# One gate's tile is computed ahead of the factor of the low-rank keys, in place of the attention's filling

## The chip, the cores and the metric

The kernel runs on one core of a Trainium2 chip. Five engines work side by side, each through its own queue in order: TensorE (PE) multiplies, its weight loads (PEld) overlap the products; VectorE (DVE) and ScalarE (ACT) do elementwise work; GpSimd (POOL) does a little; SyncE (SP) issues the transfers. They wait for each other at semaphores. The metric is the device time of one execution in microseconds.

## The reference

Two layers of an encoder trunk on 512 tokens of width 1024, in float32. Cut to what matters here:

```python
h = rms_norm(x, norm_mix[l])
u = h @ w_in[l]                    # queries, keys, values of three attentions, low-rank paths, gates
ya = prefix_block_attention(qa, ka, va, True, cum_logf)         # branch 0
qb = rms_norm(qd, mla_q_norm[l]) @ w_q_up[l]
kvb = rms_norm(kvd, mla_kv_norm[l]) @ w_kv_up[l]                # keys and values from 256 features
yb = prefix_block_attention(q_mla, k_mla, vb, False)            # branch 1
yc = chunk_band_attention(qc, kc, vc, rel_bias[l])              # branch 2
proj = einsum('bsnc,ncd->bsnd', y, w_branch[l])
gates = sigmoid(gl + b_gate[l])    # gl: 3 x 1024 columns of u
x = x + (gates * proj).sum(2) @ w_out[l]
h = rms_norm(x, norm_ffn[l])
x = x + square(relu(h @ w_ff1[l])) @ w_ff2[l]
```

## The kernel before, in words

**Products.** A float32 operand is split into a rounded high part and the rest: weights into `whi` (a copy by ACT, L142) and `wlo` (a subtraction by DVE, L143), and each product is three passes of TensorE, high by high, high by low, low by high. A weight tile of 128x1024 arrives in `raw` (L139, a load by SP). `raw`, `whi` and `wlo` have a ring of three buffers each, so a new tile can be copied only when the products of an older one are done.

**One layer.** The mixer runs the attention of branch 0, then of branch 2, then of branch 1 (the low-rank one), and after each attention its branch products `ps_b` (L803). The feed-forward part follows.

**Filling.** An attention is a generator that yields between its steps: scores S (`ps_s`, L683), probabilities P (transposes `ps_p` L713, copied by ACT to `pth` L715, low half by DVE to `ptl` L716), values V (`ps_y`, L726), transposes T (`ps_q`, L585, copied by ACT L587 and DVE L588 to `st`). It yields an amount of time, and `fill.run` takes that much of work that does not depend on it: the gate tiles. A gate tile (`gate`, by `win_tile`) is eight steps of three products (`ps_f`, L334), 650 ns of debt each, and behind the last an evacuation (DVE L778, ACT L779) and a store to `gd`. Branch 1's attention has eight such tiles; `ready` scales its debts so that eight tiles just fill it. The last head's steps have a larger weight (`tail`), so the end is filled most.

**The low-rank stage.** Before that attention its queries and keys are made, and the third branch's products (of branch 2) are woven in. The order is written out by hand as a string, `TUNE["mla"]`, one letter after the other: d and u are the low-rank tiles of queries and of keys (two steps for a letter), 0 and 1 the two scale factors, q and k the products from the low-rank features to queries, and to keys and values (`ps_t`, L369), b the branch products, t one step of the attention ahead of time (its first two are the transposes of queries and of keys), g one step of filling. It is read by these lines:

```python
            for c in TUNE["mla"]:
                if c == "t":
                    next(at)
                elif c == "g":
                    fill.run(650.0)
                elif c in "01":
                    self.mla_factor(int(c), st)
                    work["qk"[int(c)]] = (self.mla_q, self.mla_kv)[int(c)](l, st), 3 - int(c)
                else:
                    for _ in range(work[c][1]):
                        next(work[c][0], None)
```

A factor (`mla_factor_`, L478 on) is a sum over features on TensorE (`ps_sum`, L294), then some twelve small operations of DVE that end in `mf` (L485). The evacuation of a queries' or keys' tile (ACT L492 and L494, DVE L496) needs `mf`. When all four keys' tiles are evacuated, DVE makes a scale from their sums (L536, then the steps of `rsqrt`, L253 to L257) and multiplies the keys by it (L542); then they are transposed (the second t). The values' tiles, from the same products, are evacuated by ACT L412 and DVE L413. The branch products' results are taken by DVE L811 and L812.

**Order.** TensorE follows the program's order. On the other engines a scheduler sorts the instructions by priority when the program is built; after that each queue is fixed.

**Start.** `TUNE["warm"]` products of 128 columns (`ps_warm`, L1018) run while the first loads arrive.

Of the kernel before, what the change touches and what calls it, by code (L numbers as in the profile page):

```python
# [59 lines left out]
KTAGS = ("y", "s", "s", "mm")  # L60
TUNE = dict(

    mla='ddddddddddddubuubu0qqqbbqqqqqbbuuuubqbbb1kbbktkkkbbbkkkbtbbgg',

    over=[1.0, 1.0, 1.0],

# [1 line left out]

    tv=[13, 24],

    warm=15,

    st=[0, 2, 4],

# [1061 lines left out]
```

## Time and profile before

| | us |
|---|---|
| median of 3 runs | 1815.14 |
| lowest and highest | 1812.81, 1815.45 |
| the profiled execution, its time | 1812.97 |
| the profiled execution, its span | 1811.2 |
| PE busy | 1790.6 (99%) |
| DVE busy | 1078.2 (60%) |
| ACT busy | 783.8 (43%) |
| POOL busy | 88.8 (5%) |

The mean granted clock of TensorE is 0.997 of full speed. Times in the rows are microseconds from the start of the span. In a timeline an instruction is listed with its start and its length; a matrix product's listed end is modelled and overlaps the next one, so the distance of two starts is what a product takes of PE. A bracket behind a row tells how long the engine was idle before it, and what ended that.

### The profile page before, as it was taken

The numbers are of one execution on the slowest core, as the hardware profiler recorded it, in microseconds if no ns is written. First come the engines' busy times: TensorE is split into PE (matmuls) and PEld (weight loads), VectorE is DVE, ScalarE is ACT, GpSimd is POOL, SyncE is SP. The second block draws the span as 40 slices with busy tenths as digits, with TensorE's granted clock in tenths as the row PEclk, the third lists the DMA queues.
The fourth block names the chain that finished last, engine by engine and source line by source line (L and its number), as shares of the span: only waits on it lengthen the run. The fifth ranks groups of instructions, "written<-read, shape, count | busy, mean of one in ns | idle before, by whom it ended". The sixth has DMA issues, their size and how long they took to land.

```text
span 1811.2 us, 23256 instructions
## 1 busy us (share of the span) xinstructions
PE 1790.6 (99%) x8526; PEld 1493.9 (82%) x8526; DVE 1078.2 (60%) x2132; ACT 783.8 (43%) x1369; POOL 88.8 (5%) x119
## 2 busy tenths in 40 slices
PE   9999999999999999999999999999999999999999
PEld 8888888878888888888888888888788888888887
DVE  7675577597775533454356756775977655335531
ACT  6565456446643222223245744665466432212221
POOL 1021000000011000000110200000000110000000
PEclk9999999999999999999999999999999999999999
DMA  5664375332353333333336633753324433333331
GB/s 185 156 171 123 95 187 154 115 104 91 117 166 94 95 103 93 95 103 111 112 114 157 175 110 106 181 160 119 90 91 141 139 94 96 102 93 97 102 116 59
DMA packets 84224, 217.84 MB, mean 120 GB/s; under 512 B 13696, under 2 KB 16768, under 8 KB 84112
## 3 DMA queue, kind: packets, MB, share of 16 engines
q1 hardware_dynamic: 84112, 216.37, 41.3%
q8 instruction: 67, 1.10, 0.2%
q14 instruction: 45, 0.37, 0.1%
HBM read 178.44 MB, written 12.71 MB: 106 GB/s over the span
## 4 chain that ended last, share of the span: by engine, by line
PE 94%; DVE 2%; DMA 2%; ACT 1%; SPq 1%; issue 1%; POOL 0%; DVEq 0%; ACTq 0%; POOLq 0%
PE ps L334 38%; PE ps_f L334 16%; PE ps_t L369 16%; PE ps_b L803 7%; PE ps_o L334 5%; PE ps_s L683 4%; PE ps_y L726 3%; PE ps_p L713 3%; PE ps_q L585 1%; SPq L600 1%; DMA t<-rows 1%; DMA kl<-nat 1%; PE ps_k L351 0%; ACT whi L142 0%; PE ps_sum L294 0%
## 5 line engine op out<-in xcount | busy, mean ns | idle before, releaser
L142 ACT ACTIVATE whi<-raw 128x1024 fp32r<-128x1024 f32 (+1 forms) x337 | 307.1, 919 | 742.4 <-issue 297.9
L143 DVE TENSOR_TENSOR wlo<-raw,whi 128x1024 fp32r<-128x1024 f32 (+1 forms) x337 | 353.4, 1053 | 233.2 <-ACT whi L142 217.5
L334 PE MATMUL ps<-xgh,whi 128*128 128x512 f32 x512 | 199.4, 389 | 0.0
L334 PE MATMUL ps<-xgh,wlo 128*128 128x512 f32 x512 | 199.2, 389 | 0.0
L334 PE MATMUL ps<-ah,whi 128*128 128x512 f32 x512 | 199.2, 389 | 0.0
L334 PE MATMUL ps<-al,whi 128*128 128x512 f32 x512 | 199.2, 389 | 0.0
L334 PE MATMUL ps<-ah,wlo 128*128 128x512 f32 x512 | 199.2, 389 | 0.0
L334 PE MATMUL ps<-xgl,whi 128*128 128x512 f32 x512 | 199.2, 389 | 0.0
L334 PE MATMUL ps_f<-xgh,whi 128*128 128x512 f32 x464 | 195.7, 422 | 0.0
L334 PE MATMUL ps_f<-xgh,wlo 128*128 128x512 f32 x464 | 182.3, 393 | 0.0
L334 PE MATMUL ps_f<-xgl,whi 128*128 128x512 f32 x464 | 182.1, 392 | 0.0
L369 PE MATMUL ps_t<-whi,xgh 128*128 128x512 f32 x384 | 150.6, 392 | 0.0
L369 PE MATMUL ps_t<-wlo,xgh 128*128 128x512 f32 x384 | 149.7, 390 | 0.0
L369 PE MATMUL ps_t<-whi,xgl 128*128 128x512 f32 x384 | 149.6, 390 | 0.0
L334 PEld LDWEIGHTS ps<-ah,whi 128*128 128x128 f32 x512 | 96.1, 188 | 20.0
L334 PEld LDWEIGHTS ps<-ah,wlo 128*128 128x128 f32 x512 | 96.1, 188 | 20.0
L334 PEld LDWEIGHTS ps<-xgh,whi 128*128 128x128 f32 x512 | 96.1, 188 | 20.0
L334 PEld LDWEIGHTS ps<-xgl,whi 128*128 128x128 f32 x512 | 96.1, 188 | 19.9
L334 PEld LDWEIGHTS ps<-xgh,wlo 128*128 128x128 f32 x512 | 96.1, 188 | 19.9
L334 PEld LDWEIGHTS ps<-al,whi 128*128 128x128 f32 x512 | 96.1, 188 | 19.8
L957 DVE SCALAR_TENSOR_TENSOR t<-ps,rb 128x512 f32<-128x512 f32 x64 | 43.9, 691 | 113.7 <-PE ps L334 111.2
L716 DVE TENSOR_TENSOR ptl<-ps_p,pth 128x512 fp32r<-128x512 f32 x144 | 85.7, 599 | 39.1 <-ACT pth L715 38.0
(191 smaller groups left out, 3110.3 us busy)
## 6 DMA issues: line engine op xcount, KB each, us to landing
raw<-w SPq DMA_DIRECT2D x277, 512.0 KB
qq<-nat SPq DMA_DIRECT2D x64, 128.0 KB
kk<-nat SPq DMA_DIRECT2D x64, 128.0 KB
kl<-nat SPq DMA_DIRECT2D x64, 128.0 KB
gd<-t SPq DMA_DIRECT2D x32, 256.0 KB
t<-rows SPq DMA_DIRECT2D x48, 128.0 KB
cb<-cum SPq DMA_DIRECT2D x16, 256.0 KB
cb<-gd SPq DMA_DIRECT2D x16, 256.0 KB
```

Source lines behind the costliest of these rows:

```text
L142: nc.scalar.activation(out=hi[:, c : c + v], in_=raw[:, c : c + v], func=AF.Copy)
L143: nc.vector.tensor_tensor(out=lo[:, c : c + v], in0=raw[:, c : c + v], in1=hi[:, c : c + v].bitcast(F32), op=ALU.subtract)
L334: nc.tensor.matmul(out=ps, lhsT=a[:, k], rhs=b[k], start=first and k == 0 and j == 0, stop=last and k == n - 1 and j == 2)
L369: nc.tensor.matmul(out=pss[t][:, 0:width], lhsT=a[k][:, t * P : t * P + P], rhs=b[:, i], start=c == 0 and i == 0 and j == 0, stop=last and ...
L585: nc.tensor.transpose(ps[0:rows, t * P : (t + 1) * P], src(t), self.ident)
L600: nc.sync.dma_start(out=s[rows, u].bitcast(F32), in_=x[own].bitcast(F32))
L683: nc.tensor.matmul(out=ps[:, 0:n], lhsT=a[:, i * P : (i + 1) * P], rhs=b[:, 0:n], start=j == 0, stop=j == len(terms) - 1)
L713: nc.tensor.transpose(ps[:, o + (i - kb) * P : o + (i - kb + 1) * P], pr[:, offs[i] + kb * P : offs[i] + (kb + 1) * P], self.ident)
L716: nc.vector.tensor_tensor(out=pl[:, 0:w], in0=ps[:, 0:w], in1=ph[:, 0:w].bitcast(F32), op=ALU.subtract)
L726: nc.tensor.matmul(out=yps[:, kb * P : T], lhsT=qkv[2][kb // 2][:, kb % 2, h, :], rhs=head[h][gi][x][:, o : o + T - kb * P], start=gi == 0 ...
L803: nc.tensor.matmul(out=pss[u], lhsT=chunk[a][:, u, k], rhs=y[b][k], start=k == 0 and j == 0, stop=k == 3 and j == 2)
L957: nc.vector.scalar_tensor_tensor(out=t, in0=ps, scalar=0.0, in1=self.rb, op0=ALU.max, op1=ALU.mult)
```

## The change

In the string `mla`, eight letters g are put between the third group of branch products and the factor 1, and the two g at the end are taken away. Eight steps are one whole gate tile. The attention's filling then has seven tiles, and as the debts stay scaled to eight, it runs out earlier: the six steps that no longer stand in the attention are missing at its end. One warm-up product is taken away. The same string is used in both layers.

```diff
-    mla='ddddddddddddubuubu0qqqbbqqqqqbbuuuubqbbb1kbbktkkkbbbkkkbtbbgg',
+    mla='ddddddddddddubuubu0qqqbbqqqqqbbuuuubqbbbgggggggg1kbbktkkkbbbkkkbtbb',
...
-    warm=15,
+    warm=14,
```

How this moves the instructions is shown at three places of layer 0 (layer 1 has the same order). Numbers behind names tell instances apart, and they differ between the two programs.

**First place, ahead of the keys' factor.** TensorE before: a branch product, the factor's sum, the keys' first tile.

```order
L803 MATMUL ps_b_4003<-yh_3504,wlo_3995 128x512
L294 MATMUL ps_sum_4016<-ones_102,pr_3624 128x2 x4
L369 MATMUL ps_t_4055<-whi_4050,st_3679 128x512
L369 MATMUL ps_t_4055<-whi_4050,st_3680 128x512
L369 MATMUL ps_t_4055<-wlo_4051,st_3679 128x512
```

TensorE after (of the gate's 24 products the first three and the last):

```order
L803 MATMUL ps_b_4002<-yh_3503,wlo_3994 128x512
L334 MATMUL ps_f_4021<-xgh_131,whi_4016 128x512
L334 MATMUL ps_f_4021<-xgl_132,whi_4016 128x512
L334 MATMUL ps_f_4021<-xgh_131,wlo_4017 128x512
...
L334 MATMUL ps_f_4021<-xgh_178,wlo_4017 128x512
L294 MATMUL ps_sum_4050<-ones_102,pr_3623 128x2 x4
L369 MATMUL ps_t_4089<-whi_4084,st_3678 128x512
```

A whole gate tile, `ps_f_4021`, stands between the branch product and the sum. VectorE at the same place before (`tok` L569 to L577 is the queries' rotary work):

```order
L571 TENSOR_TENSOR tok_3709<-tok_3709,fqv_3941 128x8x32
L482 SCALAR_TENSOR_TENSOR mv1_4021<-ps_sum_4016,r21_4022 128x4
L577 TENSOR_TENSOR tok_3708<-tok_3708,t2_3966 128x8x32
L483 TENSOR_SCALAR mv1_4021<-mv1_4021 128x4
L574 TENSOR_TENSOR t2_3973<-tok_3709,rtab_420 128x8x16
...
L143 TENSOR_TENSOR wlo_4051<-raw_4049,whi_4050 128x1024
```

and after:

```order
L571 TENSOR_TENSOR tok_3708<-tok_3708,fqv_3940 128x8x32
L577 TENSOR_TENSOR tok_3707<-tok_3707,t2_3965 128x8x32
L574 TENSOR_TENSOR t2_3972<-tok_3708,rtab_419 128x8x16 x2
L143 TENSOR_TENSOR wlo_4017<-raw_4015,whi_4016 128x1024
...
L143 TENSOR_TENSOR wlo_4085<-raw_4083,whi_4084 128x1024
L577 TENSOR_TENSOR tok_3708<-tok_3708,t2_3979 128x8x32
L811 SCALAR_TENSOR_TENSOR cb_3998<-cb_3998,ps_b_4002 128x512
L482 SCALAR_TENSOR_TENSOR mv1_4055<-ps_sum_4050,r21_4056 128x4
L778 TENSOR_TENSOR t2_4046<-ps_f_4021,rb_397 128x512
```

The gate's split stands ahead of the factor's chain, the keys' split (`wlo_4051` before, `wlo_4085` now) too, and the gate's evacuation is inside the chain.

**Second place, from the keys' tiles to the first scores.** ScalarE before, from the copy of the second keys' weights on (`st_4098` is the queries' transposed tile):

```order
L142 ACTIVATE whi_4146<-raw_4145 128x1024
L492 ACTIVATE tok_4040<-ps_t_4055,mf1_4023 128x8x64
L494 ACTIVATE t2_4066<-ps_t_4055,mf1_4023 128x512
L142 ACTIVATE whi_4166<-raw_4165 128x1024
L492 ACTIVATE tok_4040<-ps_t_4056,mf1_4023 128x8x64
L494 ACTIVATE t2_4091<-ps_t_4056,mf1_4023 128x512
L587 ACTIVATE st_4098<-ps_q_4100,vec_85 96x512
```

and after, from the copy of the first keys' weights on:

```order
L142 ACTIVATE whi_4084<-raw_4083 128x1024
L142 ACTIVATE whi_4180<-raw_4179 128x1024
L779 ACTIVATE t2_4046<-t2_4046,hb_214 128x512
L142 ACTIVATE whi_4200<-raw_4199 128x1024
L587 ACTIVATE st_4132<-ps_q_4134,vec_85 96x512
L492 ACTIVATE tok_4074<-ps_t_4089,mf1_4057 128x8x64
L494 ACTIVATE t2_4100<-ps_t_4089,mf1_4057 128x512
```

The copy of the next branch weights and the queries' copy L587 now stand ahead of the first keys' evacuation. TensorE at the keys' transposes before:

```order
L585 MATMUL ps_q_4229<-ident_207,tok_4040 96x128 x2
L585 MATMUL ps_q_4229<-ident_207,tok_4041 96x128 x2
L334 MATMUL ps_f_4244<-xgh_132,whi_4239 128x512
...
L334 MATMUL ps_f_4244<-xgh_137,wlo_4240 128x512
L683 MATMUL ps_s_4253<-st_4227,st_4098 128x512
L683 MATMUL ps_s_4253<-st_4228,st_4098 128x512
```

and after:

```order
L803 MATMUL ps_b_4224<-yh_3503,wlo_4201 128x512
L585 MATMUL ps_q_4263<-ident_206,tok_4074 96x128 x2
L585 MATMUL ps_q_4263<-ident_206,tok_4075 96x128 x2
L683 MATMUL ps_s_4274<-st_4261,st_4132 128x512
L683 MATMUL ps_s_4274<-st_4262,st_4132 128x512
L683 MATMUL ps_s_4274<-st_4261,st_4133 128x512
```

The six gate products between transposes and scores are gone.

**Third place, the attention's end.** TensorE before, the last head (of each gate step only the first product is shown where two or three follow):

```order
L713 MATMUL ps_p_5184<-ident_207,pr_5079 128x128 x4
L334 MATMUL ps_f_5175<-xgh_137,whi_5168 128x512
...
L713 MATMUL ps_p_5202<-ident_207,pr_5079 128x128 x4
L334 MATMUL ps_f_5175<-xgh_164,whi_5168 128x512
...
L726 MATMUL ps_y_5214<-pth_5189,v_4042 128x512
L726 MATMUL ps_y_5214<-ptl_5190,v_4042 128x512
L334 MATMUL ps_f_5175<-xgh_169,whi_5168 128x512
...
L726 MATMUL ps_y_5214<-pth_5207,v_4042 128x384
```

and after:

```order
L713 MATMUL ps_p_5199<-ident_206,pr_5107 128x128 x4
L334 MATMUL ps_f_5094<-xgh_178,whi_5087 128x512
...
L713 MATMUL ps_p_5215<-ident_206,pr_5107 128x128 x4
L726 MATMUL ps_y_5224<-pth_5204,v_4076 128x512
L726 MATMUL ps_y_5224<-ptl_5205,v_4076 128x512
L726 MATMUL ps_y_5224<-pth_5220,v_4076 128x384
L726 MATMUL ps_y_5224<-pth_5220,v_4077 128x128
L713 MATMUL ps_p_5232<-ident_206,pr_5107 128x128 x2
L726 MATMUL ps_y_5224<-ptl_5221,v_4076 128x384
```

Of the seven gate steps from the first of these rows to the branch products one is left.

## Rows read from the trace of the kernel before

**Rows 1.** Who waited for whom, PE: total us, times, longest us.

```profile
PE ps_t L369 <- DVE wlo L143: 8.4, 2, 4.2
PE ps_s L683 <- DMA kl<-nat: 4.0, 4, 1.0
```

**Rows 2.** Timeline of PE, layer 0: start us, length us, engine, line, operation.

```profile
379.03 0.39 PE L803 MATMUL ps_b<-yh,wlo 128*128 128x512 f32 x1
379.26 0.95 PE L294 MATMUL ps_sum<-ones,pr 128*128 128x2 f32 x8
380.06 0.72 PE L369 MATMUL ps_t<-whi,st 128*128 128x512 f32 x2
384.99 0.79 PE L369 MATMUL ps_t<-wlo,st 128*128 128x512 f32 x1 [4.21 <-DVE wlo L143]
...
390.20 0.62 PE L369 MATMUL ps_t<-whi,st 128*128 128x512 f32 x2
```

**Rows 3.** Timeline of PE at the same place in layer 1.

```profile
1277.58 0.95 PE L294 MATMUL ps_sum<-ones,pr 128*128 128x2 f32 x8
...
1289.83 0.62 PE L369 MATMUL ps_t<-whi,st 128*128 128x512 f32 x2
```

**Rows 4.** Stretches: from and to, us, PE busy, granted clock, DMA, GB/s.

```profile
80.00:82.00 2.00, 1.61 (x7) 1.00 0.95 175
386.00:387.00 1.00, 1.00 (x4) 0.50 0.74 168
```

**Rows 5.** Timeline of DVE at the place of rows 2.

```profile
379.68 0.42 DVE L571 TENSOR_TENSOR tok<-tok,fqv 128x256 f32<-128x256 f32 x1
...
380.32 0.41 DVE L577 TENSOR_TENSOR tok<-tok,t 128x256 f32<-128x256 f32 x1
...
380.72 0.29 DVE L574 TENSOR_TENSOR t<-tok,rtab 128x128 f32<-128x128 f32 x1
...
383.71 1.23 DVE L143 TENSOR_TENSOR wlo<-raw,whi 128x1024 fp32r<-128x1024 f32 x1
```

**Rows 6.** Timeline of ACT: a weight copy, and one of eight keys' copies.

```profile
373.79 1.06 ACT L142 ACTIVATE whi<-raw 128x1024 fp32r<-128x1024 f32 x1 [4.45 <-PE ps_f L334]
...
395.75 0.67 ACT L492 ACTIVATE tok<-ps_t,mf 128x512 f32<-128x512 f32 x1
```

**Rows 7.** Timeline of PE, the keys' transposes and the first scores.

```profile
405.64 0.60 PE L585 MATMUL ps_q<-ident,tok 128*96 128x128 f32 x4
...
408.11 0.73 PE L683 MATMUL ps_s<-st 96*128 96x512 f32 x2 [0.25 <-DVE st L588]
```

**Rows 8.** Timeline of DVE, from the keys' sums to their transposes.

```profile
397.63 0.74 DVE L413 SCALAR_TENSOR_TENSOR v<-ps_t,mf,v 128x512 fp32r<-128x512 f32 x1
398.29 0.17 DVE L536 TENSOR_SCALAR fkk<-msk 128x32 f32<-128x32 f32 x1
...
401.73 2.50 DVE L542 TENSOR_TENSOR tok<-tok,rs_y 128x512 f32<-128x512 f32 x4
...
407.31 0.74 DVE L588 SCALAR_TENSOR_TENSOR st<-ps_q,vec,st 96x512 fp32r<-96x512 f32 x1
```

**Rows 9.** Timeline of PE, the last head of branch 1's attention.

```profile
484.69 0.60 PE L713 MATMUL ps_p<-ident,pr 128*128 128x128 f32 x4
...
488.34 0.40 PE L726 MATMUL ps_y<-pth,v 128*128 128x512 f32 x1
...
491.85 0.40 PE L803 MATMUL ps_b<-yh,whi 128*128 128x512 f32 x1
```

**Rows 10.** Timeline of DVE and of ACT there.

```profile
485.26 1.23 DVE L143 TENSOR_TENSOR wlo<-raw,whi 128x1024 fp32r<-128x1024 f32 x1 [0.50 <-ACT whi L142]
...
486.49 0.60 ACT L715 ACTIVATE pth<-ps_p 128x512 fp32r<-128x512 f32 x1
```

**Rows 11.** Timeline at the program's start: warm-up products, and a weight load's wait.

```profile
1.00 5.90 PE L1018 MATMUL ps_warm<-ones 128*128 128x128 f32 x30 [1.00 <-POOL ones L1012]
...
13.25 0.19 PEld L369 LDWEIGHTS ps_t<-whi,xgl 128*128 128x128 f32 x1 [0.37 <-DVE xgl L275]
```

## Prediction

> **What bounds the kernel now.** I read three views, in this order. The page gives TensorE (PE) 99% of the span: 1790.6 of 1811.2 us. So nothing but PE's own waits and its clock can move the time, unless PE's work changes, and here all but one warm-up product stays. The view of who waited for whom, kept to PE, is therefore the list of what can be won [rows 1]. Its largest entry is 8.4 us in two waits, one in each layer, and both stand where the change cuts in. The third view is PE's timeline there: the low-rank keys' factor starts at 379.26, two products of the keys follow at 380.06, the third only at 384.99 [rows 2]. It needs the low half `wlo` of the keys' weights, which VectorE (DVE) wrote from 383.71 to 384.94 [rows 5]. The weights and their high half had long been there; DVE's queue had put rope work and the factor's chain ahead of the split. After the wait PE ran at half clock, 0.50 [rows 4].
>
> What this stall costs: from 379.26 to 390.20 PE does the factor's 0.80 us and 18 products. A product starts 0.227 us after the one before at full clock [rows 2], so 18 take 4.08. 10.94 - 4.88 leaves 6.06 us lost. In layer 1 the same work goes from 1277.58 to 1289.83 [rows 3]: 12.25 - 4.88 = 7.37. The wait itself, 384.99 - 380.06 less two products, is 4.47 in each; the rest, 1.59 and 2.90, is the half clock. Some 0.25 us more is waited per layer at the first scores [rows 7]. So 6.31 and 7.62 us, 13.9 together, is what the change has to play with.
>
> **The change part by part.** Both layers have the same order of instructions after the change, so I work out layer 0 on the clock of before and use it twice. An instruction of DVE or ScalarE (ACT) that does not wait starts about 0.08 us before the listed end of the one ahead of it (1.14 for a 1.23 us split).
>
> *The gate's eight steps ahead of the factor.* 24 products of 0.227 us are moved, not added. PE reaches them at 379.26 and the third needs the gate's own `wlo`. On DVE that split now stands behind one L577 and two L574 that follow the L571 of 379.68, with no factor ahead of it: 379.68 + 0.34 + 0.33 + 2 x 0.20 = 380.76, done at 381.99 [rows 5]. The third product starts at 382.04 in place of 379.71: **2.33 us lost**, in place of 4.47. Does the clock fall? A wait of 1.02 us left it at 1.00 in the stretch around it, the one of 4.2 us did not [rows 1, 4]. PE stands still for 2.2 us here, nearer to the short one, so I take no half clock, and keep 1.59 to 2.90 as the other end.
>
> *The keys behind it.* The gate hides the keys' split: DVE reaches it at 385.46 and ends at 386.69, and PE wants it at 388.4. But the gate also brings a weight tile more into the ring of three. PE: gate to 387.1, factor to 387.9, the first keys' tile and twelve branch products to 391.98. On ACT the copy `whi` for the next branch chunk now stands ahead of the queries' copy L587 and of the first keys' copy L492. It overwrites the chunk that those twelve products read, so ACT's queue stands until 391.9, then needs 1.0 us [rows 6]. The queries' transposes end at 393.94; L587 runs 394.0 to 394.7 on ACT and its low half L588 on DVE to 395.4 [rows 8]; the factor's last operation is queued behind that and ends at 395.57. So the first L492 starts at 395.6. Two copies of 0.67 [rows 6] free the bank that PE wants at 396.52: they end at 396.86, **0.38 lost**.
>
> Eight such copies end at 400.3, and the last sum on DVE at 400.95. Before, DVE needed 3.44 us from there to the keys' scaling L542 [rows 8]. Now four L413 of 0.66, a split of 1.14 and half a split of 0.6 stand between: 7.8, less some 0.3 that fills the chain's own gaps. So L542 starts at 408.5, and its four instructions end at 411.0. PE, with 48 products after 396.9, is at the keys' transposes at 407.85. They then end their issue at 411.1 in place of 408.2: **2.9 lost**. Here before had no wait.
>
> *The two steps taken from ahead of the first scores.* Before, six gate products (1.36 us) lie between these transposes and the scores, and 0.25 is still waited [rows 7]. Without them the copy (0.68) and the low half (0.74, behind half a split) are bare: transposes end at 411.3, copy at 412.0, low half at 412.84, and the second score product waits until 412.88 in place of 411.34: **1.54 lost**.
>
> *The six steps taken from the end of the attention.* From the last head's first transposes to the first output-branch product took 7.16 us with seven steps in it [rows 9]. Six steps of 0.68 fewer leave 3.08 of work. Now the chain sets it: the first copy of probabilities ends at 485.98, a weight copy of 0.97 stands behind it on ACT, the second ends at 487.4. DVE then has a split of 1.14 ahead of the last low half (0.42) [rows 10]. The last value product starts at 489.67 and the branch at 489.79, 5.10 us after the start: **2.0 lost**. Bounds: 0, if splits come early, and 3.2, if the second copy's chain slips by another split.
>
> *Warm-up.* One product of fifteen, 5.90 / 15 = 0.39 us [rows 11]. PE would start earlier by it, but the weights' stage waits for `xgl` at 13.25 anyway, so I take 0; bounds are 0.39 won, and nothing lost, since no waiting time of DMA or split depends on it.
>
> *DMAs.* The gate's 512 KB load takes the place in SyncE's queue that the keys' had, and its store of 256 KB stands ahead of three weight loads that are not wanted for 15 us: nothing.
>
> Sum per layer after: 2.33 + 0.38 + 2.9 + 1.54 + 2.0 = 9.15 us lost, against 6.31 and 7.62 before. The change costs 2.84 + 1.53 = **4.4 us**. The profiled execution has a time of 1812.97 us (span 1811.2), so 1817.4; it lies 2.2 below the median of the runs, 1815.14, so as a median of runs 1819.5.
>
> The Trainium skill has a rule that speaks against this change ("TensorE: Matmul & The Clock Gate", section "A second HAM failure mode: psum-queue depth-cycling"): where PE idles for short times between groups of products, often enough, its clock goes down and up again. By that rule the places at 408 to 413 would run on at 1.2 GHz and the sum would be some 9 us; by the rows it needs one long wait. The trace shows no row of several short waits close together, so it decides neither way; this is the first rival.
>
> **The rivals.**
> *Half clock after the transposes.* From 408.1 to 412.9 PE does no more than four transposes and one product. Before, 4.2 us with nothing brought the level of 1.2 GHz, in both layers, and cost 1.59 and 2.90. For it: the stretch is longer. Against it: it is not empty, and no pause in it passes 1.2 us. Price 1.59 + 2.90 = 4.5 on top: 1824.0.
>
> *The keys' scale is there in time (not slower).* If ACT is not held at the branch's weight copy, the first L492 starts earlier. The price falls us by us from 0.38 + 2.9, and from 3.3 us earlier on nothing of it is left: 4.4 - 2 x 3.3 = -2.2, so 1812.9. With the end's 2.0 gone too it is -6.2, 1808.9. For it: which buffer the copy gets is my reading of which tile is freed first, though the wait of 4.45 us of such a copy before, which ended with the last product of the up tile, fits it [rows 6]. Against it: the L587 and L588 in both queues ahead of the copies hold them to 395.4 by themselves, since the queries' transposes come after the second keys' tile on PE.
>
> *It is a swap.* The gate's split waits as long as the keys' did, 4.47, because DVE or the load is later than I add. Then the early place costs 2.14 more with 1.59 to 2.90 of half clock: 1819.5 + 4.3 + 4.5 = 1828.3. Against it: the rows ahead of the split are the same, in the same order, less the factor's.
>
> **How the numbers follow.** My forecast has a chance of 0.48, with a range of its own of 1816 to 1823 (a microsecond or two on each of the two largest terms). The half clock has 0.28, the scale in time 0.16 (0.08 of it with the end's wait gone), the swap 0.04, and 0.04 is for gate steps that meet other splits inside the attention, within 2 us of no change. About 0.2%, 3.6 us, is what a measurement of this kernel can tell from no change: 1811.5 to 1818.8. Slower: 0.29 of the forecast's 0.48, 0.28 and 0.04 = 0.61. Faster: the 0.08. The rest, 0.31, is within. The range, 1812.5 to 1826, leaves out the faster end and the swap.
>
> **What would show it.** Right: PE's waits for `wlo` fall to some 2 us each and move to `ps_f` L334, at clock 1.00; new waits of 2 to 3 us for `tok` L542 at `ps_q` L585, of 1 to 1.5 at `ps_s` L683, and several of 0.3 to 1 at `ps_y` L726 by the last head; ACT idle before a `whi` copy until a branch product is done. Wrong: no wait at L585, which is the largest term; then the time is that of before or less. A granted clock of 0.5 after the first scores is the first rival. A tail that ends without waits takes 4 us off.

## The result, and the profile after

| | before | after |
|---|---|---|
| median of 4 runs, us | 1815.30 | 1829.69 |
| lowest and highest, us | 1812.81, 1816.28 | 1829.16, 1830.88 |
| span of the profiled execution, us | 1811.2 | 1829.1 |
| mean granted clock of TensorE in it | 0.997 | 0.994 |

The change makes the kernel slower by 14.4 us by the medians, a ratio of 1.0079; the recorded ratio is 1.0088, with a 95% interval of 1.0076 to 1.0100. The forecast was 4.4 us more than the median then known, with a range that ended at 1826. The sign and the places were right; the size was a third of what was measured. One execution of the kernel with 14 warm-up products (3643 us, the profiled one) and one of the kernel with only the keys' split moved (2763 us) lie far off all others, and the ratios leave them out.

First, who waited for whom on PE in the changed kernel (total us, times, longest us), to be set against [rows 1]:

```profile
PE ps_q L585 <- DVE tok L542: 4.6, 8, 1.4
PE ps_f L334 <- DVE wlo L143: 4.3, 2, 2.1
PE ps_s L683 <- DMA kl<-nat: 4.0, 4, 1.0
PE ps_y L726 <- DVE ptl L716: 2.3, 6, 0.5
PE ps_p L713 <- DVE nat L588: 2.0, 2, 1.5
PE ps_s L683 <- ACT st L587: 1.5, 2, 0.8
...
PE ps_t L369 <- ACT t L494: 0.5, 2, 0.3
```

The 8.4 us for `wlo` at L369 are gone. In their place stand the four waits that the prediction named: the gate's own `wlo`, the keys' scale at the transposes, the scores, the value products. The third row is the same as before and has nothing to do with the change. Nor has the fifth: its wait of 1.5 us stands in the first attention of layer 1, where the profiled execution of the changed string with 15 warm-up products has none.

PE's timeline of layer 0 at the three places, to be set against [rows 2], [rows 7] and [rows 9]:

```profile
380.41 0.39 PE L334 MATMUL ps_f<-xgl,whi 128*128 128x512 f32 x1
382.94 0.50 PE L334 MATMUL ps_f<-xgh,wlo 128*128 128x512 f32 x1 [2.15 <-DVE wlo L143]
...
412.23 0.28 PE L585 MATMUL ps_q<-ident,tok 128*96 128x128 f32 x1 [1.37 <-DVE tok L542]
412.83 0.28 PE L585 MATMUL ps_q<-ident,tok 128*96 128x128 f32 x1 [0.32 <-DVE tok L542]
...
415.10 2.00 PE L683 MATMUL ps_s<-st 96*128 96x512 f32 x3 [0.78 <-ACT st L587]
416.90 0.63 PE L334 MATMUL ps_f<-xgh,whi 128*128 128x512 f32 x1
...
421.92 0.52 PE L683 MATMUL ps_s<-st 96*128 96x256 f32 x3
...
495.26 0.60 PE L713 MATMUL ps_p<-ident,pr 128*128 128x128 f32 x4
...
500.35 0.38 PE L726 MATMUL ps_y<-ptl,v 128*128 128x256 f32 x1 [0.54 <-DVE ptl L716]
500.57 0.40 PE L803 MATMUL ps_b<-yh,whi 128*128 128x512 f32 x1
```

Behind the scores a gate product is listed with 0.63 us in place of 0.39, and these products start 0.43 us apart. That is half clock, and the stretches show it, to be set against [rows 4] (from and to, us, PE busy, granted clock, DMA, GB/s):

```profile
382.00:384.00 2.00, 1.06 (x4) 0.90 0.07 10
384.00:386.00 2.00, 2.00 (x7) 0.50 0.79 252
414.00:416.00 2.00, 1.19 (x3) 0.58 0.04 8
416.00:418.00 2.00, 2.00 (x5) 0.50 0.84 250
418.00:420.00 2.00, 2.00 (x7) 0.50 0.03 12
1292.00:1294.00 2.00, 2.00 (x6) 0.50 0.88 238
1324.00:1326.00 2.00, 2.00 (x5) 0.50 0.82 199
```

While PE still had work, the clock went down to 1.2 GHz four times in this execution, twice in each layer: behind the gate's wait, and behind the keys' transposes. The prediction's sum had it down nowhere.

Last, ACT and DVE on the way to the keys' scale, the part of the sum that rested on reading queues:

```profile
394.69 1.06 ACT L142 ACTIVATE whi<-raw 128x1024 fp32r<-128x1024 f32 x1 [2.50 <-PE ps_b L803]
396.71 0.68 ACT L587 ACTIVATE st<-ps_q,vec 96x512 fp32r<-96x512 f32 x1 [0.96 <-PE ps_q L585]
398.37 0.69 ACT L492 ACTIVATE tok<-ps_t,mf 128x512 f32<-128x512 f32 x1 [0.97 <-DVE mf L485]
```

```profile
397.53 0.74 DVE L588 SCALAR_TENSOR_TENSOR st<-ps_q,vec,st 96x512 fp32r<-96x512 f32 x1
398.19 0.15 DVE L485 TENSOR_TENSOR mf<-rs_y,rtok 128x4 f32<-128x4 f32 x1
...
404.40 0.17 DVE L536 TENSOR_SCALAR fkk<-msk 128x32 f32<-128x32 f32 x1
...
411.40 2.48 DVE L542 TENSOR_TENSOR tok<-tok,rs_y 128x512 f32<-128x512 f32 x4
```

It went as forecast, step by step: the weight copy waits for the branch products, L587 and L588 come next, `mf` is queued behind L588, the first L492 waits for `mf`, and the scaling L542 starts 13.0 us after that first copy, where the sum had 12.9. That the two agree so closely is partly luck: the operation behind the last sum (L536) comes 6.0 us after the copy and not 5.35, and the scaling 7.0 after that and not 7.5.

The terms beside each other, in us per layer. Each is the distance of two starts in PE's timeline, less the work between them at full clock (0.227 us for a product of 512 columns):

| term | forecast | layer 0 | layer 1 |
|---|---|---|---|
| gate's wait for its `wlo` | 2.33 | 2.30 | 2.31 |
| half clock behind it | 0 | 1.75 | 1.73 |
| bank of the first keys' tile | 0.38 | 0.42 | 0.42 |
| wait at the keys' transposes | 2.9 | 3.07 | 3.07 |
| waits at the first scores | 1.54 | 1.52 | 1.5 |
| half clock from there on | 0 | 2.43 | 2.4 |
| the attention's last head | 2.0 | 2.23 | 2.24 |
| elsewhere in the attention, and the branch products behind it | 0 | 1.0 | 0.6 |
| sum | 9.15 | 14.7 | 14.3 |
| lost there before | | 6.31 | 7.62 |

The scores and the half clock behind them together are 3.95 us in layer 0: from the end of the transposes, 414.13, to the scores of 256 columns at 421.92 are 7.79 us, and 3.84 of them are work. What the waits alone cost is read from a kernel below in which the clock stayed up: 1.52. The two layers give 14.7 + 14.3 - 13.9 = 15.1 us. The two profiled executions differ by 17.9 us in their spans; the other 2.8 lie outside these places, most of them in the wait of 1.5 us named above and in a start that was later by 0.8. The medians differ by 14.4: the profiled execution of before, 1812.97 us, lies 2.3 below its median, and that of the changed kernel, 1830.88, lies 1.2 above.

### The profile page after: what moved, and what is told of

Read it like the earlier page. It is cut to its first block, busy times and chain, and to the rows that moved or that the text cites. A ratio compares the mean times of both kernels' runs of the same rounds, so it can differ in the third digit from the quotient of the medians.

```text
span 1829.1 us, 23256 instructions
## 1 busy us (share of the span) xinstructions
PE 1801.0 (98%) x8524; PEld 1496.8 (82%) x8524; DVE 1077.3 (59%) x2130; ACT 785.7 (43%) x1367; POOL 89.2 (5%) x119
## 4 chain that ended last, share of the span: by engine, by line
PE 91%; DVE 3%; DMA 2%; ACT 2%; SPq 1%; issue 1%; POOL 0%; DVEq 0%; ACTq 0%
PE ps L334 38%; PE ps_f L334 16%; PE ps_t L369 15%; PE ps_b L803 6%; PE ps_o L334 5%; PE ps_s L683 4%; PE ps_y L726 3%; PE ps_p L713 3%; PE ps_q L585 1%; SPq L600 1%; DVE wlo L143 1%; DMA t<-rows 1%; ACT whi L142 1%; DMA kl<-nat 1%; PE ps_k L351 0%
## 5 line engine op out<-in xcount | busy, mean ns | idle before, releaser
L369 PE MATMUL ps_t<-whi,xgh 128*128 128x512 f32 x384 | 150.7, 392 | 0.3 <-ACT whi L142 0.3
L369 PE MATMUL ps_t<-wlo,xgh 128*128 128x512 f32 x384 | 149.9, 390 | 0.4 <-DVE wlo L143 0.4
L369 PE MATMUL ps_t<-whi,xgl 128*128 128x512 f32 x384 | 149.6, 389 | 0.0
L334 PEld LDWEIGHTS ps_f<-xgh,wlo 128*128 128x128 f32 x464 | 88.4, 191 | 25.3 <-DVE wlo L143 5.1
```

The costliest lines, as they stand in the source:

```text
L334: nc.tensor.matmul(out=ps, lhsT=a[:, k], rhs=b[k], start=first and k == 0 and j == 0, stop=last and k == n - 1 and j == 2)
L369: nc.tensor.matmul(out=pss[t][:, 0:width], lhsT=a[k][:, t * P : t * P + P], rhs=b[:, i], start=c == 0 and i == 0 and j == 0, stop=last and ...
```

## The experiments

Each kernel below ran on a chip with the kernel before beside it, whose median there was 1813.3 to 1813.8 us and not 1815.3. So the fair measure between them is the excess over that median: 14.4 us for the changed kernel.

**Which part of the change it is.** Two kernels take the two numbers of the change apart. First the warm-up alone:

```diff
-    warm=15,
+    warm=14,
```

> The kernel before with 14 warm-up products in place of 15, nothing else. Theory A (the warm-up is worth nothing): within 0.5 us of before, at most 0.39 us either way. Rival B (the 0.79 us by which the changed kernel is already late at the first factor's sum, 24.16 in place of 23.37, comes from the missing product): 0.8 us slower, and the sum at 24.2.

Measured: 1813.96 us beside 1813.79 of the kernel before on the same chip, a ratio of 0.9999 (0.9990 to 1.0008). Theory A got its number, though an interval of some 1.6 us to either side does not exclude 0.8. Against theory B speaks the next kernel: it has all 15 products, and its first sum starts at 24.16 too. So the 0.8 us by which the changed kernel was late there is one execution against another.

Then the string alone, with `warm=15`:

> The change to the order of the low-rank stage alone, with the 15 warm-up products of before. Theory A: the time of the whole change, 1829.7 us within 0.5, since all of it lies in that stage and at the attention's end. Rival B: 0.8 us below the whole change, 1828.9.

Measured: 1829.37 us, 15.6 above the kernel before, ratio 1.0086 (1.0073 to 1.0100). The loss lies in the string. Its profiled execution had a surprise. In layer 0 it has the same wait for the gate's `wlo`, 2.16 us, but no half clock behind it; in layer 1 the half clock is there:

```profile
380.00:382.00 2.00, 0.48 (x2) 1.00 0.00 0
382.00:384.00 2.00, 2.00 (x11) 1.00 0.66 188
384.00:386.00 2.00, 2.00 (x11) 1.00 0.37 101
...
1290.00:1292.00 2.00, 2.00 (x6) 0.50 0.42 150
```

**Is the half clock the cause of what the sum lacked?** The hole is the stretch at the keys' transposes, from the last branch product to the first scores, in which PE mostly waits. Two kernels fill it with products of 128 columns that nobody reads. In the string a w is one of them:

```diff
-kkkbtbb
+kkkbwwwwtwwbb
...
+    def hold(self, n):
+        ps = self.pt.tile([P, T], F32, tag="pt", name="ps_hold")
+        for _ in range(n):
+            self.nc.tensor.matmul(out=ps[:, 0:P], lhsT=self.ones, rhs=self.ones, start=True, stop=True)
```

> The changed kernel with six products of 128 columns into a bank that nobody reads, put into the hole at the keys' transposes: four ahead of them (about 1.5 us, the wait there is 1.37 to 1.5) and two behind them, ahead of the first scores (0.74 us, the wait there is 0.78). No other engine's order changes, so every wait for the keys' scale stays. Theory A (the half clock comes from the hole, and was the part that the sum lacked): the granted clock is 1.00 from 414 to 422, the first scores and the gate steps behind them take 0.227 us a product, and each layer gets 2.4 to 3.0 us back: 1824.3 us. Rival C (the waits themselves are the loss, and what PE does in them does not matter): the clock is 0.5 there as before and the time 1829.7, or up to 0.5 more.

Measured: 1827.59 us, 13.8 above the kernel before, with executions from 1823.89 to 1830.44, ratio 1.0073 (1.0060 to 1.0085). In the profiled one, the fastest, the clock fell behind the transposes of layer 0 and not of layer 1:

```profile
414.00:416.00 2.00, 2.00 (x6) 0.50 0.89 258
1316.00:1318.00 2.00, 1.31 (x7) 1.00 0.00 0
1318.00:1320.00 2.00, 1.72 (x7) 1.00 0.42 76
```

The executions reach from theory A's number to rival C's, and the median is neither's. Between the transposes there still were four waits of 0.3 to 0.4 us, so the six products left a stretch of 2 us with little in it. So the hole was filled whole, with eleven ahead and five behind:

> As the kernel with six products into a bank that nobody reads, but with eleven ahead of the keys' transposes (3.2 us at the 0.29 us that they took there) and five between them and the first scores (1.4 us), so that TensorE stands still nowhere from 408 to 414. The order of the other engines is that of the changed kernel. Theory A (the clock falls where TensorE does little for 2 to 4 us, four separate transposes in it do not count, and a full stretch keeps it): the granted clock is 1.00 from 410 to 422 in both layers, the mean clock 0.997 to 0.998, and the time 4.8 us below the changed kernel, 1824.5. Rival C (what TensorE does there does not matter): 0.5 from 412 on as with the six, 1829.5.

Measured: 1826.41 us, 13.1 above the kernel before, ratio 1.0073 (1.0060 to 1.0086). The clock of the hole and what follows, in both layers:

```profile
410.00:412.00 2.00, 2.00 (x17) 1.00 0.00 0
412.00:414.00 2.00, 1.94 (x15) 1.00 0.00 0
414.00:416.00 2.00, 1.82 (x10) 1.00 0.38 55
416.00:418.00 2.00, 2.00 (x11) 1.00 0.51 207
...
1316.00:1318.00 2.00, 2.00 (x17) 1.00 0.03 8
1320.00:1322.00 2.00, 1.88 (x10) 1.00 0.72 190
```

It is 1.00 there throughout, and from the first scores to those of 256 columns PE takes 3.83 us (415.59 to 419.42) in place of 6.82. So the half clock is there because PE does little in the hole. Of the 3.0 us, 2.4 are the half clock, as in theory A, and the rest is the wait for the low half, which the five products behind the transposes cover. The gain is smaller than 4.8 because the sixteen products are too many: from the end of the last branch product to the scores they take 5.8 us where the waits and transposes took 4.4. 3.0 less 1.4 is 1.6 us a layer, 3.1 in both. The times alone do not show it: the excess is 13.1 us beside 14.4 and, for the string alone, 15.6, and the three intervals overlap. It is the trace that decides here: unfilled and with the long wait ahead of it, the hole was followed by half clock six times of six (the changed kernel, the string alone, the stretched filling below), and filled whole never in four (this kernel and one below). In the same execution the clock still fell behind the gate's wait in both layers, and once behind the last head, at 1403.7 in layer 1.

**Are the losses separate, or does one only move to the next place?** The gate's split earlier on VectorE, by a higher priority of the gate's load and split at that place:

```diff
                 elif c == "g":
-                    fill.run(650.0)
+                    self.early(fill)
...
+    def early(self, fill):
+        self.ahead += 14
+        fill.run(650.0)
+        self.ahead -= 14
```

> The changed kernel, with the gate tile ahead of the factor loaded and split at a priority higher by 14, so that its low half stands on VectorE two rope steps earlier, right behind the low half of the up tile, and the factor's chain stands earlier too. ScalarE's order stays. Theory A (each wait is a loss of its own): the 2.2 us wait and its 1.75 us of half clock go in both layers, 8 us less than the changed kernel: 1821.5. Rival E (VectorE's backlog of rope work sets when the keys' scale is there, and TensorE only comes earlier to the wait for it): the wait at the keys' transposes grows by what the first one gives back, and the time is 1826 to 1829.5.

Measured: 1819.55 us, ratio 1.0035 (1.0021 to 1.0048), 6.2 above the kernel before in place of 14.4. That is about the 8 us of theory A; rival E falls. PE waits now:

```profile
...
PE ps_t L369 <- DVE wlo L143: 3.1, 3, 1.2
PE ps_y L726 <- DVE ptl L716: 2.2, 6, 0.6
PE ps_q L585 <- DVE tok L542: 1.9, 6, 0.3
PE ps_s L683 <- ACT st L587: 1.5, 2, 0.8
...
```

The gate waits no more, a wait of up to 1.2 us for the keys' `wlo` comes up, and at the transposes only the short waits between them are left: the scaling starts 21.1 us behind the factor's sum in place of 21.7, and PE comes 0.9 us later, held up by the new wait. In layer 0 the clock stayed at 1.00 behind the transposes; in layer 1 it fell with the same waits:

```profile
1314.00:1316.00 2.00, 2.00 (x6) 0.50 0.00 0
```

So in layer 0 the waits at the first scores can be read alone: the last transpose at 410.51, the scores of 256 columns at 415.96, 5.36 us behind its end where 3.84 is work.

Then six steps of the gate ahead of the factor, and two kept between the transposes and the scores:

```diff
-bbbgggggggg1kbbktkkkbbbkkkbtbb
+bbbgggggg1kbbktkkkbbbkkkbtbbgg
```

> The changed kernel with six of the eight gate steps ahead of the factor and two at the string's end, where the kernel before has them, between the keys' transposes and the first scores. The attention's end still has the six steps fewer. On ScalarE the copy of the next branch weights no longer stands ahead of the first keys' copies. Theory A (the lateness of the keys' scale comes from that copy on ScalarE, as in the prediction's sum): no wait at the keys' transposes, none at the first scores, no half clock there: the 3.1, 1.5 and 2.4 us go in both layers, 14 us less, 1815.5. Rival F (the scale is late by VectorE's queue, whatever ScalarE does): the wait of 2 to 3 us at the transposes stays, only the scores' wait goes, 1822 to 1826.

Measured: 1821.78 us, 8.5 above the kernel before, ratio 1.0045 (1.0031 to 1.0059). No wait at the transposes is left, so F is wrong on that: the first copy L492 starts 4.8 us behind the factor's sum in place of 8.7, and the scaling 17.0 in place of 21.7. Only 1.4 us of these 4.7 are won up to L536. The other 3.3 lie between it and the scaling, on VectorE, where in the changed kernel one and a half weight splits and three value tiles stood between and now none do. The edit moved both queues, so how much either does by itself is not shown. The time is near F's, since another wait came up, for the bank that VectorE frees with a value tile's low half:

```profile
PE ps_f L334 <- DVE wlo L143: 4.3, 2, 2.1
...
PE ps_t L369 <- DVE v L413: 2.8, 2, 1.4
...
PE ps_s L683 <- DVE st L588: 1.3, 4, 0.5
```

At the attention's end the filling was stretched to the seven tiles that are there:

```diff
-    over=[1.0, 1.0, 1.0],
+    over=[1.0, 0.875, 1.0],
```

> The changed kernel with the debts of the low-rank attention scaled to seven gate tiles in place of eight (0.875 of before), so that its filling lasts to its end again, and each earlier place gets a little less. Theory A (the prediction's term for the attention's end is a loss of its own, measured at 2.2 us a layer in the changed kernel): the waits at the last value products go and nothing replaces them, 4.4 us below the changed kernel, 1825.2. Rival G (56 steps do not cover this attention wherever they stand): new waits inside it of the same sum, 1829.5.

Measured: 1829.57 us, 15.7 above the kernel before, ratio 1.0083 (1.0067 to 1.0098), no gain. Rival G holds:

```profile
PE ps_q L585 <- DVE ptl L716: 3.2, 4, 1.0
...
PE ps_y L726 <- DVE ptl L716: 1.0, 3, 0.5
```

Of the 2.3 us at the value products 1.3 went, and 3.2 new ones stand at transposes inside the attention. From the first scores to the first branch product behind the attention PE takes 86.0 and 85.4 us in the two layers, where the changed kernel took 85.5 and 85.3. The profiled execution is the fastest by far, at 1824.52 us, theory A's number; but there the clock had stayed up behind the gate's wait in both layers, so most of what it is below the others is luck. With 56 steps this attention is short of cover, at its end as well as with the steps spread over it.

**Where the wait of before comes from.** The kernel before, with the keys' split alone moved ahead:

```diff
-        with k.tc.high_priority(k.ahead):
+        with k.tc.high_priority(k.ahead + 10 * (key == ("kvup", 0))):
             w = n // pieces
```

> The kernel before, with one number more: the keys' weights get a higher priority by 10, which puts their low half on VectorE ahead of the factor's chain, behind the rope work at 378.3. ScalarE's order stays. Theory A (the wait and its half clock are all that is lost there, 6.06 and 7.37 us): 13.4 us less than before, 1801.9. Rival D (TensorE then comes 6 us earlier to the keys' transposes, and the keys' scale, which hangs on the factor's chain, is late for it as in the changed kernel): a wait of 2 to 3 us at the transposes, with or without half clock, 1807 to 1812.

Measured: 1814.76 us, ratio 1.0003 (0.9994 to 1.0012). Both theories are wrong. The wait for `wlo` went, and one of the same length came up four of PE's instructions later:

```profile
PE ps_b L803 <- DVE cb L811: 8.5, 2, 4.2
```

The next branch product needs a bank, and the operation that frees it stood behind the same rope work and factor's chain on VectorE, at 384.63. So that operation was moved ahead as well:

```diff
-                        nc.vector.scalar_tensor_tensor(out=g, ...
+                        with self.tc.high_priority(80 * (n == 2)): nc.vector.scalar_tensor_tensor(out=g, ...
```

> The kernel before with two numbers: the keys' weights at a priority higher by 10, and the operation with which VectorE frees the bank of a product of the third branch at one higher by 80, so that both stand ahead of the queries' rope work. Theory A (VectorE's queue order alone makes the 4.2 us, the backlog has slack behind it): no wait of more than 1 us from 378 to 410, no half clock, 13.4 us less than before: 1800.4. Rival D (the backlog itself is too long, as the kernel with the first number alone points to, where the wait of 4.2 us went from the keys' low half to the bank, 1814.8 in place of 1813.8): the wait moves on to the queries' transposes or the keys' scale, 1807 to 1814.

Measured: 1808.25 us beside 1813.31 of the kernel before, ratio 0.9972 (0.9962 to 0.9983). This kernel is faster than both. In the profiled execution its clock never falls while PE has work. The backlog comes out at a third place, later and smaller, at the queries' transposes (L585), which need the last rope operation:

```profile
385.36 0.49 PE L585 MATMUL ps_q<-ident,tok 128*96 128x128 f32 x3
387.67 0.32 PE L585 MATMUL ps_q<-ident,tok 128*96 128x128 f32 x1 [1.82 <-DVE tok L577]
```

Of the 13.4 us 5.1 came back, so rival D is right. In the profiled execution PE comes to these transposes 5.7 and 7.0 us sooner behind the factor's sum than before, and from there to the first scores it takes 2.8 us longer in each layer, 1.8 of them this wait. With these transposes two keys' tiles later (`kbbkkktk` in the string):

> The kernel with the two priorities (1808.25 us), and in the string the first t two k later (kbbkkktk in place of kbbktkkk), so that TensorE does two keys' tiles, 2.7 us, before it transposes the queries. Theory A (the wait of 1.8 us for the queries' rope work is the last of the backlog): this wait goes in both layers and nothing takes its place, 3.6 us less, 1804.6. Rival D (the chain to the keys' scale or the next bank comes next): 1806 to 1809.

Measured: 1809.62 us, ratio 0.9973 (0.9964 to 0.9982), the same as without. That is rival D, but for the place: the rope's wait is gone, and the values' weights are late in its place, with half clock behind that in layer 0.

```profile
PE ps_t L369 <- DVE wlo L143: 4.1, 2, 2.0
```

**Two that combine.** The gate's split earlier, and the hole filled with seven and five products:

> The kernel with the gate's split earlier (1819.55 us), and with seven products into a bank that nobody reads ahead of the keys' transposes and five behind them, so that no stretch is left in which TensorE does little. Theory A (what is left beyond the waits is half clock at the transposes, one layer of two in the profiled execution): granted clock 1.00 from 376 to 424 and from 1274 to 1330, mean clock 0.999 or 1.0 in every execution; the waits stay, so the time falls only by the half clock, 2 to 3 us: 1817. Rival C: some execution still has a mean clock of 0.997 or less, 1819.5.

Measured: 1820.40 us, ratio 1.0039 (1.0025 to 1.0053), 6.6 above the kernel before, where the earlier split alone had 6.2. The clock of the hole is 1.00 in both layers, and no execution has a mean below 0.998, as theory A said; but its time is missed by 3 us. A wait of 1.2 us for the keys' `wlo` was followed by half clock in layer 1, and the products overran the waits again. So this kernel tells nothing on the price of the half clock.

The changed string with two places moved ahead on VectorE, the gate's split and the third branch's banks:

> The changed kernel, with the gate's split at a priority higher by 14 and the operation that frees the third branch's banks at one higher by 80. Theory A (with VectorE's queue in order the gate tile at its new place costs nothing, but its steps are missing behind the keys' transposes and at the attention's end, 1.5 and 2.2 us a layer, and the scale is late by up to 1.5): 7 to 10 us above the kernel of before with the two priorities, 1815 to 1818. Rival H (the gate tile covers so much of VectorE's backlog that the change pays once its split is in time): 1808 or less.

Measured: 1817.19 us, ratio 1.0018 (1.0008 to 1.0029), 3.4 above the kernel before and 8.9 above the kernel of before with two priorities. Theory A's number holds and H's does not. The parts are not the forecast ones, though:

```profile
PE ps_t L369 <- DVE wlo L143: 4.9, 3, 2.3
...
```

A wait of 2.3 us for the keys' `wlo` remains in each layer, and in the profiled execution half clock follows it both times; the two executions with a mean clock of 1.000 took 1814.0 and 1814.3 us. The priority for the keys' split, which the kernel of before with two priorities has, is not in this kernel. So whether the new place would pay with that split in time as well is untested, and H is not settled.

## Why the prediction was wrong

*The queues were read rightly.* Five losses were forecast from the order of the instructions and from durations of before, and all five came within 0.25 us a layer: 2.30 for 2.33, 0.42 for 0.38, 3.07 for 2.9, 1.52 for 1.54, 2.23 for 2.0. The hold of ScalarE's weight copy behind the branch products, which the rival of the scale in time doubted, is there (2.50 us). That rival and the swap fall; whether the warm-up is worth its 0.39 us is finer than the times can tell.

*The step that failed is the clock.* The prediction asked twice whether it falls, and its sum put no half clock at either place. For the gate it compared a stand of 2.2 us with one of 1.02 after which the clock stayed up and one of 4.2 after which it fell, and took the nearer. For the transposes it argued that the stretch is not empty and that no pause in it passes 1.2 us. Both times the clock fell, and in the profiled execution the two cost 1.75 + 2.43 us a layer, 8.3 in all, beside the 10 us by which the median missed the forecast. The kernel with the filled hole shows that at the transposes it is the hole that does it. For the gate it is partly chance: behind the same wait the clock fell in six cases of twelve, as told below. The second argument was wrong in kind: four transposes of 0.09 us in more than three microseconds did not keep the clock up. The rule of the Trainium skill that the prediction set against itself ("TensorE: Matmul & The Clock Gate", section "A second HAM failure mode: psum-queue depth-cycling") would have had the clock down at the transposes, and there the trace agrees with it: 0.50 in both layers. In the two kernels with shorter waits there (six products, the gate's split earlier) it was 0.50 in one layer of two.

*The range was too narrow by the prediction's own terms.* It kept 1.59 to 2.90 us a layer as the other end for the gate, and 4.5 us for the transposes as a rival, but never added the two to its forecast. 1819.5 + 4.5 + 4.5 is 1828.5, within 1.2 us of the result. Two unknowns with the same cause are not alternatives; whoever gives one a chance of 0.28 must ask what the other does then.

*The end of the attention was short by half a microsecond to one.* The term for the last head was 2.0 and measured 2.23 us; 0.6 to 1.0 more were lost inside the attention and at the branch products behind it, where the outputs of the last head (L739, L740) come late for PE. The prediction stopped its sum at the first branch product. That the stretched filling does not help shows that the loss is the missing cover itself, and not its place.

*The price of what was there to win was read rightly, but the reason was too small.* The prediction named the place of one split in VectorE's queue as the reason for the 6.06 and 7.37 us. The kernel with that split alone moved, which gained nothing, shows that it is the backlog behind it: rope work, factor's chain, splits and banks, all wanted by PE within 5 us.

What stays open: why the branch products behind the attention wait by 0.3 us in one execution and 1.1 in another, and which part of the 8.9 us between the old and the new string, each with two priorities, is cover and which is order.

## What to carry to other kernels

A wait of PE for a busy engine is removed at the queue, not at the instruction: list everything behind it that PE wants in the next microseconds, since the next one can take its place with the same length, as here. A step that fills a wait at one place is missing at the place that it is taken from; ask there first which waits it covered. And price each stretch in which PE does little twice, as a wait and as half clock behind it, and add the prices of all such stretches for the far end of the range.

## What the runs showed of the hardware that was not expected

The same wait leaves half clock behind, or not. The gate's wait for `wlo` of 2.15 to 2.16 us stands in both layers of six kernels' profiled executions (the changed one, the string alone, the two with products in the hole, six and two, the stretched filling). Of these twelve, six were followed by a clock of 0.50 for some 3 us, at about 1.75 us lost, and six by 1.00. The wait of 4.2 us was followed by half clock four times of four, in the kernel before and in the one with the split alone moved. Single waits of other lengths: 2.3 us twice of two, 2.0 once of two, 1.4 to 1.8 never of six, 1.2 once of six, and the waits of some 1.0 us for a load never. The last head's short waits were followed by it in layer 1 of two kernels (the hole filled whole, the gate's split earlier). The Trainium skill states something that could be the reason for this chance ("TensorE: Matmul & The Clock Gate", section "What's actually happening"): the hardware judges the activity in windows that run on by themselves and do not start with the program. The traces agree in so far as the same instructions with the same waits came out both ways; no run shows the windows.

It also shows in the times. The mean granted clock was 0.994 or 0.995 in all four executions of the changed kernel, 0.996 or 0.997 in those of before beside the string alone, and 0.999 or 1.000 with the two priorities, whose eight executions lie within 2.1 us. The kernel with the hole filled by six products had 0.998 and 1823.89 us in one execution, 0.994 and 1830.44 in another. It is not all of the spread: the kernel with the earlier split and twelve products had 0.999 at 1817.05 us and 0.998 at 1825.02.
